# Border work of halves and layers in interleaved pieces, neighbouring seven-product units in alternation, last slabs in pairs

## The chip, the cores and the metric

The kernel runs on one core of a Trainium2 chip. The core has TensorE (PE, matrix products into the PSUM banks; PEld is its loading of weights), VectorE (DVE), ScalarE (ACT), GpSimd (POOL) and SyncE (SP, which issues the transfers from memory). Each engine works through its own list of instructions in order, and waits at an instruction until what it needs is there. The metric is the time of the whole program on the device in microseconds (us); lower is better.

## The reference

One inference step of a small encoder: 1024 frames of a new stream and 32 frames of a running one pass through two layers. Each layer is a mixer (Mamba-2 in the first, HGRN2 in the second) with a residual sum, then a gated feed-forward network (FFN) with a residual sum:

```python
def swiglu(h, w_gate, w_up, w_down):
    return (jax.nn.silu(h @ w_gate) * (h @ w_up)) @ w_down
...
            x = x + out.astype(x.dtype)
            x = x + swiglu(rmsnorm(x, ffn_norm_w[layer]), ffn_w_gate[layer], ffn_w_up[layer], ffn_w_down[layer])
        y = rmsnorm(x, final_norm_w)
```

The width is 1024, the FFN's hidden width 2816, all in float32. `rmsnorm` divides each frame by the root of its mean square and multiplies by a weight per channel.

## The kernel before

**Data.** The 1056 frames are two halves: h = 0 with 512 columns, h = 1 with 544, worked as two blocks of 272 (`BLK`). Channels lie on the 128 partitions, so `acc[h][m]`, m = 0 to 7, holds the residual stream. Every float32 operand is split into a rounded high part and a low rest (`xh`, `xl`; `wh`, `wl`), and a product is three matmuls: h by wh (L278), l by wh (L279), h by wl (L280). ACT makes the high part of a split by a copy, DVE the low part by a subtraction.

**The FFN.** Its hidden width is cut into eleven slabs of 256. The first slabs of a half (two of h = 0, one of h = 1) are done in the plain way (`ffn_head`: `ffn_up` twice, then `ffn_down`). The others are groups of slabs in `ffn_half`: for each slab a gate unit, then an upper unit; then the product with `w_down`, due after the next group's first gate unit. A group of two slabs (a pair) makes eight outputs of four k-steps, 12 matmuls each, where two single slabs make sixteen outputs of 6. Each output is added to `acc` by DVE (`acc<-mm,acc`), which frees its PSUM bank.

**A unit** (`ffn_unit`, `unit_weights`, `part`; L906 to L908) computes two blocks of 128 hidden channels by seven products of half the size in place of eight, with sums of the weights and of the inputs. Each of the parts p1, p5, p6, p3, p7, p2, p4 is 12 matmuls of half the columns (256 or 272). p1, p6, p7 and p4 go one after another into one PSUM bank, `px`, and between them ACT copies its state out (`s<-mm`); p5 and p3 go into `py`, p2 into `pz`. The sums of the weights are made on DVE as a unit goes on; its 1 MB of weights lands in a buffer of its own for one unit, and in two of the three `raw` buffers for the next. All other weights use those three as well.

**Border work.** Before a half's units can run, three things are needed: `x_stat` (the squares of `acc` on ACT, their sum on DVE, a product with ones on PE at L295, then rstd on ACT, kept in `rkeep`), the normed and split input (`xf`, then `h` and `l`), and `x_combos`, which makes from the channels k and k + 4 the sums for the seven products (`xt`) and splits them (`th`, `tl`). For the second half `x_combos` does the norm too.

**What sets the order.** A scheduler lists the instructions of each engine in the order of the program, except that work marked as raised moves ahead: `x_stat` and `x_combos` carry `@lifted("norm")`, a priority raised by 600. PSUM tiles come from a ring of five (`mm`) and a ring of three (`sc`); a product waits until the tile five, or three, before its own has been emptied. SP issues transfers in its list's order too, and waits when the buffer of one isn't free.

Of the kernel before, what the change touches and what calls it, by code (L numbers as in the profile page):

```python
# [47 lines left out]
def trunk_kernel(ctx, tc, x_prompt, x_sample, state_ssd, cache_conv, state_hgrn,  # L48
# [26 lines left out]
    def psum_mm():  # L75
        return pm.tile([P, 512], F32, tag="mm", bufs=5, name=nm("mm"))
# [751 lines left out]
    @lifted("norm")  # L828
    def x_stat(h, tag):

        keep = T(tag, "rkeep")
        return rstd_of([acc[h][m][:, :LEN[h]] for m in range(KD)], BLK[h], 1.0 / D, LEN[h], keep)

    @lifted("norm")
    def x_combos(h, wc, xn, tx, r=None):
# [3 lines left out]
        for k in range(4):  # L839
            xf = []  # L840
            for m in (k, k + 4):
                f = T("n", "xf")
                if xn[m] is not None:
                    tt(f[:, :L], xn[m][0].bitcast(F32)[:, :L], xn[m][1].bitcast(F32)[:, :L], ADD)
                else:
                    stt(f[:, :L], acc[h][m][:, :L], vc[:, wc + m:wc + m + 1], r[:, :L], MUL, MUL)
                    xn[m] = split(f[:, :L], L, (T("xn", "h", F32R), T("xn", "l", F32R)))
                xf.append(f)
# [6 lines left out]
            for q, f in enumerate((t, u)):  # L855
                tags = [XN2[4 * k + 2 * q], XN2[4 * k + 2 * q + 1]]
                tx[2 * k + q] = split(f[:, :L], L, (T(tags[0], "th", F32R), T(tags[1], "tl", F32R)))

# [17 lines left out]
    def unit_weights(src):  # L876
# [33 lines left out]
    def ffn_unit(h, src, xn, tx, dst):  # L910

        n = LEN[h] // 2
        w1, w5, w6, w3, w7, w2, w4 = unit_weights(src)
# [14 lines left out]
        part(py, n, w3, of(xn[4:], 1), True)  # L928
        tt(dst[0][:, hi], py[:, :n], s12[:, hi], ADD)
        part(px, n, w7, of(t34, 0), True)  # L930
        act(s35[:, lo], px[:, :n], AF.Copy)
        part(pz, n, w2, of(xn[4:], 0), False)
        tt(dst[0][:, lo], pz[:, :n], s12[:, lo], ADD)
        tt(dst[1][:, hi], s35[:, lo], s35[:, hi], ADD)
        part(px, n, w4, of(t34, 1), True)
        act(dst[1][:, lo], px[:, :n], AF.Copy)

    def ffn_gate(layer, h, s, xn, tx, g):
        L = LEN[h]
        g += [T("w", "fg") for _ in range(2)]  # L940
        ffn_unit(h, ffn_w_gate[layer][:, s * 256:(s + 1) * 256], xn, tx, g)
        for x in g:
            t = T("w", "ft")
            act(t[:, :L], x[:, :L], AF.Tanh, scale=0.5)
            stt(x[:, :L], t[:, :L], 1.0, x[:, :L], ADD, MUL)

    def ffn_upper(layer, h, s, xn, tx, g, hid):
        L = LEN[h]
        u = [T("xd", "fu") for _ in range(2)]
        ffn_unit(h, ffn_w_up[layer][:, s * 256:(s + 1) * 256], xn, tx, u)  # L950
        for x, y in zip(g, u):
            stt(y[:, :L], x[:, :L], 0.5, y[:, :L], MUL, MUL)
            hid.append(split(y[:, :L], L, (T("ys", "fh", F32R), T("ys", "fl", F32R))))
# [20 lines left out]
    def ffn_down(layer, h, s, hid, blocks=None, mid=None):  # L974
# [13 lines left out]
        if blocks is None:  # L988
            for c in range(nk):
                w = load(c)  # L990
                for m in range(c * cols // P, (c + 1) * cols // P):
                    for (b0, bn) in BLK[h]:
                        out(w, m, b0, bn)
# [7 lines left out]

    def ffn_head(layer, h, s, xn):

        hid = []
        return [lambda i=i: ffn_up(layer, h, s, i, hid, xn) for i in range(2)] + \
               [lambda: ffn_down(layer, h, s, hid)]
# [23 lines left out]
    def mixer_ffn(mixer, layer, wc, nxt):  # L1030
# [10 lines left out]
        for t in rest:  # L1041
            t()
# [126 lines left out]
```

## Time and profile before

| what | value |
|---|---|
| time, three runs | 3002.16, 2997.96, 2999.59 us (median 2999.59) |
| the profiled execution | 2997.74 us, its span 2996.0 us |
| PE busy | 2874.4 us (96%) |
| DVE busy | 2221.6 us (74%) |
| ACT busy | 1560.8 us (52%) |
| mean granted clock of the PE | 0.988 |

The rows shown further on come from the page of one profiled execution (busy times, groups of instructions, transfers) and from views of its trace: what an engine waited for (total us, times, longest), the timeline (start, length, engine, line, operation, output and inputs, shapes, count, and in brackets the idle time before it with what ended it), and stretches of the span with busy times by engine and the granted clock. L12 is line 12 of the kernel. Places on the timeline are us from the start of the span. Successive instructions overlap by a little, so the time between two starts is shorter than one's length.

In order of time the FFN of the first layer is at 930 to 1630 us (half border near 1250), that of the second at 2270 to 2950 (half border near 2585); the mixers lie before each.

### The profile page before, as it was taken

Reading aid. Unit: us, or ns where it says so; the run is one execution under the profiler, and the core shown is the slowest. Engines: PE = TensorE matmul, PEld = TensorE weight load, DVE = VectorE, ACT = ScalarE, POOL = GpSimd, SP = SyncE. Lnnn points to the kernel's source line nnn. Section 1 sums busy time; section 2 is a strip of 40 time slices with the busy share of each in tenths; the row PEclk is TensorE's granted clock in tenths of the full one; section 3 lists DMA queues with packets and bytes.
Section 4 is the critical chain, followed back from the end, with each engine's and each line's share of the span. In section 5 each row is a group of like instructions: output and inputs, shape, how many; then the busy total and the mean of one; then the engine's idle time right before and its main releaser. Section 6 shows DMA issues by size and latency. Waiting matters only on the chain.

```text
span 2996.0 us, 49501 instructions
## 1 busy us (share of the span) xinstructions
PE 2874.4 (96%) x19655; PEld 2625.4 (88%) x19655; DVE 2221.6 (74%) x3863; ACT 1560.8 (52%) x2928; POOL 51.9 (2%) x156
## 2 busy tenths in 40 slices
PE   7999999999998999899999999999999999899998
PEld 6777778989987998799999888899988999799998
DVE  6877787777787977977778555655568878787777
ACT  6745545553643644544444555655565545454445
POOL 0000000000100000000000000000000000000000
PEclk9999999999999999999999999999999999999999
DMA  5443324343332333222332222222222323333223
GB/s 143 121 109 102 99 71 127 107 114 96 100 97 78 105 114 92 89 81 87 112 92 76 85 78 81 68 76 76 77 77 91 113 85 99 95 99 92 85 88 106
DMA packets 398275, 283.42 MB, mean 95 GB/s; under 512 B 28873, under 2 KB 380634, under 8 KB 398042
## 3 DMA queue, kind: packets, MB, share of 16 engines
q1 hardware_dynamic: 398042, 280.25, 32.3%
q8 instruction: 154, 2.52, 0.4%
q14 instruction: 79, 0.65, 0.1%
HBM read 272.39 MB, written 7.82 MB: 94 GB/s over the span
## 4 chain that ended last, share of the span: by engine, by line
PE 71%; DVE 13%; DMA 7%; ACT 6%; issue 2%; SPq 0%; DVEq 0%; POOL 0%; ACTq 0%; POOLq 0%
PE mm L278 16%; PE mm L280 16%; PE mm L279 16%; PE mm L906 5%; PE mm L907 5%; PE mm L908 5%; DMA cumB<-cumd 2%; DMA raw<-in_ffn_w_gate_dram 2%; DVE wh L85 2%; ACT wh L82 1%; DMA raw<-in_ffn_w_up_dram 1%; ACT cumB L82 1%; PE sc L505 1%; PE sc L295 1%; PE sc L516 1%
## 5 line engine op out<-in xcount | busy, mean ns | idle before, releaser
L82 ACT ACTIVATE wh<-raw 128x512 fp32r<-128x512 f32 (+1 forms) x688 | 561.3, 819 | 762.9 <-PE mm L279 602.7
L278 PE MATMUL mm<-h,wh 128*128 128x272 f32 (+2 forms) x2064 | 676.0, 329 | 8.5 <-ACT h L82 4.0
L280 PE MATMUL mm<-h,wl 128*128 128x272 f32 (+2 forms) x2064 | 669.6, 325 | 2.7 <-DVE wl L85 2.7
L279 PE MATMUL mm<-l,wh 128*128 128x272 f32 (+2 forms) x2064 | 668.6, 324 | 1.2 <-DVE l L85 0.9
L85 DVE TENSOR_TENSOR wl<-raw,wh 128x1024 fp32r<-128x1024 f32 x308 | 376.3, 1223 | 141.5 <-ACT wh L82 123.5
L278 PEld LDWEIGHTS mm<-h,wh 128*128 128x128 f32 x2064 | 390.2, 189 | 39.3 <-ACT h L82 5.1
L280 PEld LDWEIGHTS mm<-h,wl 128*128 128x128 f32 x2064 | 390.6, 189 | 33.3 <-DVE wl L85 4.0
L279 PEld LDWEIGHTS mm<-l,wh 128*128 128x128 f32 x2064 | 390.6, 189 | 31.4 <-DVE l L85 3.0
L85 DVE TENSOR_TENSOR acc<-mm,acc 128x272 f32<-128x272 f32 (+1 forms) x544 | 278.3, 527 | 164.6 <-PE mm L280 162.4
L278 PE MATMUL mm<-fh,wh 128*128 128x272 f32 (+1 forms) x1056 | 346.0, 328 | 22.0 <-DVE acc L85 20.4
L906 PE MATMUL mm<-th,wh 128*128 128x272 f32 (+1 forms) x1216 | 351.8, 289 | 7.2 <-ACT s L82 6.6
L280 PE MATMUL mm<-fh,wl 128*128 128x272 f32 (+1 forms) x1056 | 343.9, 326 | 5.8 <-DVE wl L85 5.8
L907 PE MATMUL mm<-tl,wh 128*128 128x272 f32 (+1 forms) x1216 | 346.0, 285 | 0.0
L908 PE MATMUL mm<-th,wh 128*128 128x272 f32 (+1 forms) x1216 | 345.7, 284 | 0.0
L279 PE MATMUL mm<-fl,wh 128*128 128x272 f32 (+1 forms) x1056 | 345.2, 327 | 0.0
L85 DVE TENSOR_TENSOR wh<-raw,wh 128x512 fp32r<-128x512 f32 x380 | 257.2, 688 | 30.5 <-ACT wh L82 27.8
L906 PEld LDWEIGHTS mm<-th,wh 128*128 128x128 f32 x1216 | 228.7, 188 | 18.4 <-ACT s L82 18.1
L278 PEld LDWEIGHTS mm<-fh,wh 128*128 128x128 f32 x1056 | 200.7, 190 | 38.7 <-ACT wh L82 21.2
L908 PEld LDWEIGHTS mm<-th,wh 128*128 128x128 f32 x1216 | 229.1, 188 | 0.0
L907 PEld LDWEIGHTS mm<-tl,wh 128*128 128x128 f32 x1216 | 228.8, 188 | 0.0
L280 PEld LDWEIGHTS mm<-fh,wl 128*128 128x128 f32 x1056 | 201.1, 190 | 23.2 <-DVE wl L85 7.6
L279 PEld LDWEIGHTS mm<-fl,wh 128*128 128x128 f32 x1056 | 201.3, 191 | 15.5 <-DVE fl L85 0.5
(256 smaller groups left out, 5504.3 us busy)
## 6 DMA issues: line engine op xcount, KB each, us to landing
raw<-in_ffn_w_down_dram SPq DMA_DIRECT2D x90, 512.0 KB, 3.5
raw<-in_ffn_w_gate_dram SPq DMA_DIRECT2D x88, 512.0 KB, 4.8
raw<-in_ffn_w_up_dram SPq DMA_DIRECT2D x88, 512.0 KB, 3.8
raw<-in_ssd_in_w_dram SPq DMA_DIRECT2D x80, 512.0 KB, 4.5
raw<-in_hgrn_in_w_dram SPq DMA_DIRECT2D x64, 512.0 KB, 4.2
cumB<-cumd SPq DMA_DIRECT2D x64, 256.0 KB, 4.0
raw<-in_ssd_out_w_dram SPq DMA_DIRECT2D x32, 512.0 KB, 3.9
raw<-in_hgrn_out_w_dram SPq DMA_DIRECT2D x16, 512.0 KB, 3.3
```

The costliest lines, as they stand in the source:

```text
L82: A.activation(out=out, in_=in_, func=f, **kw)
L85: (eng or V).tensor_tensor(out=out, in0=a, in1=b, op=op)
L278: PE.matmul(ps[:, :bn], a, mh, start=(k == 0), stop=False)
L279: PE.matmul(ps[:, :bn], a, ml, start=False, stop=False)
L280: PE.matmul(ps[:, :bn], b, mh, start=False, stop=(k == n - 1))
L295: PE.matmul(ps[:, :bn], ones, tot[:, b0:b0 + bn], start=True, stop=True)
L505: PE.matmul(pp, Btok[:n, :], xw[:n, :], start=True, stop=True)
L516: PE.matmul(y13[r:r + 64, i // 2, :n], xdt[:n, i * 64:(i + 1) * 64], cums[i // 4][:n, i % 4, :n], start=True, stop=True)
L906: PE.matmul(ps[:, :n], a, mh, start=(k == 0 and not more), stop=False, skip_group_check=True)
L907: PE.matmul(ps[:, :n], a, ml, start=False, stop=False, skip_group_check=True)
L908: PE.matmul(ps[:, :n], b, mh, start=False, stop=(k == 3), skip_group_check=True)
```

## The change

1. `x_stat` and `x_combos` lose the raised priority. The norm of the second half leaves `x_combos` and becomes `norm_pieces`, one piece for a channel block and a block of columns. `x_combos`, `ffn_outs` (the outputs of `ffn_down`) and `ffn_head` return lists of pieces too; `mixed` interleaves two lists, `run` runs one. `x_stat` of the next half is called by `hook`, in the second group's first gate unit, after the outputs of the group before.
2. A unit becomes a generator that stops five times: p1 | p5, p2 | p6, p3 | p7 | p4 with what follows the unit. `in_turn` runs two neighbouring units A and B in the order A3 B1 A4 B2 A5, then B3 C1 B4 C2 B5, and so on. The sums of weights are made part by part. `px` comes from two `mm` banks of its own, `py` and `pz` from the `sc` ring of three, the outputs from the other three `mm` banks.
3. The last two slabs of a half are one pair, except at the end of the program, where they stay two singles.

```diff
-    def psum_mm():
-        return pm.tile([P, 512], F32, tag="mm", bufs=5, name=nm("mm"))
+    def psum_mm(among=(0, 1, 2, 3, 4)):
+        turn[0] += 1
+        i = among[turn[0] % len(among)]
+        return pm.tile([P, 512], F32, tag=f"mm{i}", bufs=1, name=nm("mm"))
...
-    @lifted("norm")
     def x_stat(h, tag):
...
-    @lifted("norm")
-    def x_combos(h, wc, xn, tx, r=None):
+    def norm_pieces(h, wc, out, blocks, r):
+
+        def piece(m, b0, bn):
+            xf = T("n", "xf")
+            stt(xf[:, :bn], acc[h][m][:, b0:b0 + bn], vc[:, wc + m:wc + m + 1], r[:, b0:b0 + bn], MUL, MUL)
+            if m == len(out):
+                out.append((T("xn", "h", F32R), T("xn", "l", F32R)))
+            xh, xl = out[m]
+            act(xh[:, b0:b0 + bn], xf[:, :bn], AF.Copy)
+            tt(xl[:, b0:b0 + bn], xf[:, :bn], xh[:, b0:b0 + bn].bitcast(F32), SUB)
+        return [lambda m=m, b=b: piece(m, *b) for b in blocks for m in range(KD)]
...
+        px = psum_mm((0, 1))
...
-        part(px, n, w1, of(xn[:4], 0), False)
+        part(px, n, next(w), of(xn[:4], 0), False)
         act(s12[:, lo], px[:, :n], AF.Copy)
-        part(py, n, w5, of(t12, 0), False)
+        yield
+        py, pz = psum_sc(), psum_sc()
+        part(py, n, next(w), of(t12, 0), False)
         act(s35[:, hi], py[:, :n], AF.Copy)
-        part(px, n, w6, of(t12, 1), True)
+        part(pz, n, next(w), of(xn[4:], 0), False)
+        yield
...
+    def in_turn(units):
+
+        step = lambda u: u and next(u, None)
+        prev = None
+        for u in list(units) + [None]:
+            if u:
+                u = u()
+            if prev is None:
+                step(u)
+                step(u)
+            else:
+                step(prev)
+                step(u)
+                step(prev)
+                step(u)
+                step(prev)
+            prev = u
...
+            ps = psum_mm((2, 3, 4))
+            product(ps, ws[c], (m * P) % cols, hid, b0, bn)
+            accumulate(h, m, ps, b0, bn)
+        return [lambda m=m, b=b: piece(m, *b) for m in range(KD) for b in BLK[h]]
...
-        groups = [1] * (n % 2) + [2] * ((n - 2) // 2) + [1, 1] if n % 2 == 0 else \
-                 [1] + [2] * ((n - 3) // 2) + [1, 1]
...
+        n = NSLAB - first - sum(tail)
+        groups = [1] * (n % 2) + [2] * (n // 2) + tail
...
-        due = ffn_half(layer, 0, xn[0], tx[0], HEAD)
-        due[0]()
-        x_combos(1, wc, xn[1], tx[1], r)
-        due[1]()
-        for t in ffn_head(layer, 1, 0, xn[1]):
-            t()
...
+        run(mixed(rest, tc0[2:3]))
+        run(mixed(h1[2:], tc0[3:]))
+        r = []
+        due = ffn_half(layer, 0, xn[0], tx[0], HEAD, lambda: r.append(x_stat(1, "ec")), [2])
+        run(mixed(ffn_outs(*due[0]), norm_pieces(1, wc, xn[1], BLK[1], r[0])))
+        tc1 = x_combos(1, xn[1], tx[1])
+        h2 = ffn_head(layer, 1, 0, xn[1])
+        run(h2[:1] + tc1[:1] + h2[1:2] + tc1[1:2] + mixed(h2[2:], tc1[2:]))
```

**How instructions move, first place.** DVE at the half border of the first layer (`acc_0_98` to `acc_7_105` are the first half's residual, `acc_..._106` to `_113` the second's; `mm` is an output in PSUM). Before:

```order
L85 TENSOR_TENSOR xt_12963<-xf_12951 128x272
L85 TENSOR_TENSOR l_12960<-xf_12957,h_12959 128x544
L85 TENSOR_TENSOR xt_12963<-xf_12957,xt_12963 128x272
L85 TENSOR_TENSOR xt_12964<-xf_12957,xf_12951 128x272
L85 TENSOR_TENSOR xt_12964<-xf_12957,xt_12963 128x272
L85 TENSOR_TENSOR fl_12789<-fu_12658,fh_12788 128x512
L85 TENSOR_TENSOR tl_12970<-xt_12963,th_12969 128x544
L85 TENSOR_TENSOR fl_12794<-fu_12659,fh_12793 128x512
L85 TENSOR_TENSOR tl_12974<-xt_12964,th_12973 128x544
L85 TENSOR_TENSOR acc_0_98<-mm_12803,acc_0_98 128x512
L85 TENSOR_TENSOR acc_1_99<-mm_12811,acc_1_99 128x512
```

And in the changed program:

```order
L92 SCALAR_TENSOR_TENSOR xf_12881<-acc_5_111,vc,rkeep_10366 128x272
L92 SCALAR_TENSOR_TENSOR xf_12901<-acc_6_112,vc,rkeep_10366 128x272
L89 TENSOR_TENSOR acc_0_98<-mm_12803,acc_0_98 128x512
L89 TENSOR_TENSOR l_12884<-xf_12881,h_12883 128x272
L92 SCALAR_TENSOR_TENSOR xf_12907<-acc_7_113,vc,rkeep_10366 128x272
L89 TENSOR_TENSOR acc_1_99<-mm_12829,acc_1_99 128x512
L89 TENSOR_TENSOR l_12904<-xf_12901,h_12903 128x272
L89 TENSOR_TENSOR wl_12916<-raw_12913,wh_12915 128x1024
L89 TENSOR_TENSOR l_12910<-xf_12907,h_12909 128x272
L92 SCALAR_TENSOR_TENSOR xf_12933<-acc_0_106,vc,rkeep_10366 128x272
L89 TENSOR_TENSOR acc_2_100<-mm_12861,acc_2_100 128x512
```

Before, the emptying of the first `mm` (`acc_0_98<-mm_12803`) stands behind all of the second half's norm and sums; now it stands between blocks of the norm, and the sums follow later, between outputs of the head.

**Second place.** ACT in the last gate and upper units of the first half (`s<-mm` copies out a unit's `px`, `s<-sc` or `s_2060_12559<-mm_12556` its `py`; `wh` and `fh` are splits). Before:

```order
L82 ACTIVATE s_2059_12558<-mm_12555 128x256
L82 ACTIVATE s_2060_12559<-mm_12556 128x256
L82 ACTIVATE wh_12665<-raw_12660 128x512
L82 ACTIVATE s_2059_12558<-mm_12555 128x256
L82 ACTIVATE wh_12669<-s_2067_12664 128x512
L82 ACTIVATE wh_12674<-raw_12660 128x512
L82 ACTIVATE s_2060_12559<-mm_12555 128x256
L82 ACTIVATE wh_12678<-s_2067_12664 128x512
L82 ACTIVATE wh_12681<-raw_12660 128x512
```

And in the changed program (`mm_12481` is the gate unit's `px`, `mm_12619` the upper unit's):

```order
L86 ACTIVATE s_2040_12482<-mm_12481 128x256
L86 ACTIVATE wh_12694<-raw_2042_12484 128x512
L86 ACTIVATE wh_12721<-raw_12622 128x512
L86 ACTIVATE s_2060_12620<-mm_12619 128x256
L86 ACTIVATE wh_12738<-s_2064_12626 128x512
L86 ACTIVATE s_2041_12483<-mm_12481 128x256
L86 ACTIVATE wh_12754<-raw_12622 128x512
L86 ACTIVATE ft_12710<-fw_12581 128x512
L86 ACTIVATE s_2061_12621<-sc_12660 128x256
```

Before, one `px`, `mm_12555`, is copied out again and again, with one other part between two uses; now the copies of two units' `px` alternate.

**Third place.** SP, the weights of a group of the first half. Before:

```order
L94 DMA raw_12249<-in_ffn_w_down_dram 128x4x256
L94 DMA raw_1988_12117<-in_ffn_w_gate_dram 128x4x256 x2
L94 DMA raw_12283<-in_ffn_w_down_dram 128x4x256
L94 DMA raw_12317<-in_ffn_w_down_dram 128x4x256
L94 DMA raw_2047_12526<-in_ffn_w_gate_dram 128x4x256 x2
L94 DMA raw_12351<-in_ffn_w_down_dram 128x4x256
L94 DMA raw_12387<-in_ffn_w_up_dram 128x4x256
L94 DMA raw_12388<-in_ffn_w_up_dram 128x4x256
```

And in the changed program:

```order
L98 DMA raw_12213<-in_ffn_w_up_dram 128x4x256
L98 DMA raw_1983_12075<-in_ffn_w_gate_dram 128x4x256 x2
L98 DMA raw_12214<-in_ffn_w_up_dram 128x4x256
L98 DMA raw_12307<-in_ffn_w_down_dram 128x4x256
L98 DMA raw_2042_12484<-in_ffn_w_gate_dram 128x4x256 x2
L98 DMA raw_12341<-in_ffn_w_down_dram 128x4x256
L98 DMA raw_12375<-in_ffn_w_down_dram 128x4x256
L98 DMA raw_12409<-in_ffn_w_down_dram 128x4x256
L98 DMA raw_12622<-in_ffn_w_up_dram 128x4x256
```

Before, the `w_up` loads follow the `w_down` loads; now those of an upper unit stand ahead of the `w_down` loads that the gate unit before it triggers.

More of the change, by code (lines that the diff above doesn't have):

```diff
@@ L842, in x_combos @@
                 f = T("n", "xf")
[L843 to L847, printed above, removed]
+                tt(f[:, :L], xn[m][0].bitcast(F32)[:, :L], xn[m][1].bitcast(F32)[:, :L], ADD)
                 xf.append(f)
@@ L988, in ffn_down @@
         if blocks is None:
[L989 to L993, printed above, removed]
+            for t in ffn_outs(layer, h, s, hid):
+                t()
         else:
@@ L1019, in ffn_half @@
                 g = []
-                ffn_gate(layer, h, s + i, xn, tx, g)
-                if i == 0 and gi < len(groups) - 1:
-                    for d in due:
-                        d()
-                    due = []
-                ffn_upper(layer, h, s + i, xn, tx, g, hid)
-            due.append(lambda s=s, hid=hid, **k: ffn_down(layer, h, s, hid, **k))
+                before = []
+                if i == 0 and gi <= len(groups) - len(tail):
+                    before, due = due, []
@@ L1027, in ffn_half, with gate @@
+                def gate(s=s + i, g=g, before=before, gi=gi):
+                    yield from ffn_gate(layer, h, s, xn, tx, g)
+                    for d in before:
+                        run(ffn_outs(*d))
+                    if gi == 1 and before:
+                        hook()
+                units.append(lambda gate=gate: gate())
+                units.append(lambda s=s + i, g=g, hid=hid: ffn_upper(layer, h, s, xn, tx, g, hid))
+            due.append((layer, h, s, hid))
             s += ng
+        in_turn(units)
@@ L1047, in mixer_ffn @@
-        r = x_stat(1, "ec")
-        due = ffn_half(layer, 0, xn[0], tx[0], HEAD)
-        due[0]()
-        x_combos(1, wc, xn[1], tx[1], r)
-        due[1]()
-        for t in ffn_head(layer, 1, 0, xn[1]):
-            t()
-        r = nxt and x_stat(0, "ss")
-        due = ffn_half(layer, 1, xn[1], tx[1], 1)
-        return due, r
+        xn, tx = [[], []], [[None] * KD, [None] * KD]
+        h0, h1 = [ffn_head(layer, 0, s, xn[0]) for s in range(HEAD)]
+        rest = mixer([lambda: norm(0, wc, xn[0], XN)] + h0[:2])
@@ L1058, in trunk_kernel @@
+        r = []
+        due = ffn_half(layer, 1, xn[1], tx[1], 1, lambda: r.append(nxt and x_stat(0, "ss")),
+                       [2] if nxt else [1, 1])
+        return due, r[0]
     wrow = []
```

122 lines of the change are left out of this document (66 added, 56 removed).

## The prediction

> **What bounds the kernel now.** I read the busy times first, then what TensorE (PE) waited for, then the places on its timeline, then the clock.
>
> ```profile
> PE 2874.4 (96%) x19655; PEld 2625.4 (88%) x19655; DVE 2221.6 (74%) x3863; ACT 1560.8 (52%) x2928; POOL 51.9 (2%) x156
> PE mm L278 <- DVE acc L85: 23.5, 3, 10.2
> PE mm L906 <- ACT s L82: 6.6, 13, 0.9
> ```
>
> The PE is the bound: 96% of the span, no other engine over 74%. Since the change issues as many matmuls as before, of the same sizes, only its waits and its clock can move the end. The waits are few and large: the one on `acc` happens three times and costs 23.5 us. The timeline of the PE says where. A number in brackets is the wait ahead of that row and its releaser.
>
> ```profile
> 963.96 2.18 PE L295 MATMUL sc<-sq,ones 128*128 128x272 f32 x4 [10.17 <-DVE sq L85]
> 1252.97 0.76 PE L278 MATMUL mm<-fh,wh 128*128 128x512 f32 x1 [10.23 <-DVE acc L85]
> 1256.41 0.79 PE L280 MATMUL mm<-fh,wl 128*128 128x512 f32 x1 [2.24 <-DVE wl L85]
> 1625.17 0.39 PE L278 MATMUL mm<-fh,wh 128*128 128x272 f32 x1 [0.53 <-DVE fu L85]
> 1627.23 0.40 PE L278 MATMUL mm<-fh,wh 128*128 128x272 f32 x1 [1.05 <-DVE nco L1120]
> 1631.57 0.60 PE L280 MATMUL mm<-fh,wl 128*128 128x272 f32 x1 [1.32 <-DVE wl L85]
> 2280.05 0.60 PE L278 MATMUL mm<-hy,wh 128*128 128x272 f32 x1 [3.06 <-DVE acc L85]
> 2284.32 0.40 PE L280 MATMUL mm<-hy,wl 128*128 128x272 f32 x1 [0.56 <-DVE wl L85]
> 2583.16 0.77 PE L278 MATMUL mm<-fh,wh 128*128 128x512 f32 x1 [10.20 <-DVE acc L85]
> 2586.60 0.79 PE L280 MATMUL mm<-fh,wl 128*128 128x512 f32 x1 [2.24 <-DVE wl L85]
> ```
>
> Five places, each a border where norms and sums for the seven products fall due: the first layer's FFN head (964), its half border (1253), the layer border (1625), the second FFN's head (2280), its half border (2583). The ten waits add up to 41.6 us. VectorE (DVE) is what is late; its timeline at 1253 shows why.
>
> ```profile
> 1225.09 1.48 DVE L88 SCALAR_TENSOR_TENSOR xf<-acc,vc,rkeep 128x544 f32<-128x544 f32 x2
> ...
> 1237.91 0.45 DVE L85 TENSOR_TENSOR xt<-xf,xt 128x272 f32<-128x272 f32 x1
> 1238.27 0.45 DVE L85 TENSOR_TENSOR xt<-xf,xf 128x272 f32<-128x272 f32 x1
> ...
> 1251.49 0.74 DVE L85 TENSOR_TENSOR tl<-xt,th 128x544 fp32r<-128x544 f32 x1
> 1252.12 3.10 DVE L85 TENSOR_TENSOR acc<-mm,acc 128x512 f32<-128x512 f32 x5
> 1255.11 1.24 DVE L85 TENSOR_TENSOR wl<-raw,wh 128x1024 fp32r<-128x1024 f32 x1
> ```
>
> From 1225 to 1252 the DVE does the raised `x_combos` of the next half and empties none of the five `mm` banks; then it empties five in a row. The PE filled them and stood still.
>
> The clock adds to it. The columns of the stretches are length; PE, weight load, DVE, ACT and POOL busy; granted clock; DMA share and GB/s.
>
> ```profile
> 964.00:970.00 6.00, 6.00 (x16) 4.72 (x17) 3.56 (x7) 2.91 (x4) 0.00 (x0) 0.57 0.00 0
> 1252.50:1260.00 7.50, 4.78 (x12) 3.38 (x13) 7.50 (x11) 0.20 (x1) 0.00 (x0) 0.55 0.27 76
> 1626.00:1636.00 10.00, 7.63 (x40) 7.13 (x39) 9.80 (x20) 3.32 (x4) 0.00 (x0) 0.66 0.33 92
> 2279.00:2285.00 6.00, 4.38 (x21) 4.17 (x22) 5.97 (x12) 4.53 (x6) 0.00 (x0) 0.72 0.01 3
> 2582.00:2590.00 8.00, 4.60 (x10) 3.23 (x11) 8.00 (x12) 0.89 (x1) 0.00 (x0) 0.50 0.24 70
> 1000.00:1225.00 225.00, 223.94 (x1549) 206.85 (x1548) 181.94 (x298) 114.72 (x221) 0.00 (x0) 1.00 0.33 101
> 1300.00:1610.00 310.00, 306.29 (x2413) 302.53 (x2412) 238.22 (x411) 149.46 (x283) 0.00 (x0) 1.00 0.30 89
> ```
>
> Busy time times lost clock, row by row: 6.00 x 0.43 = 2.6, 4.78 x 0.45 = 2.2, 7.63 x 0.34 = 2.6, 4.38 x 0.28 = 1.2, 4.60 x 0.50 = 2.3, together 10.9 us. The borders so cost 41.6 + 10.9 = **52.5 us**. The last two rows are stretches of units: clock 1.00, and 530.2 of 535 us busy.
>
> **Part 1, the border work in pieces.** What leaves is the solid block of DVE work; the same operations come back, cut into pieces between products. For the half border I counted both written orders. Steps from start to start on the DVE, out of the rows above and the next one: a 544-wide operation 0.63 (1251.49 to 1252.12), 272 wide 0.36 (1237.91 to 1238.27), 512 wide 0.61 (a fifth of the 3.10, less the tail), a wide `wl` 1.13 (1255.11 to 1256.24); the `xf` scaling 0.74 at 544, and half, 0.37, at 272.
>
> ```profile
> 1256.24 0.71 DVE L85 TENSOR_TENSOR acc<-mm,acc 128x512 f32<-128x512 f32 x1
> ```
>
> For the matmuls two pairs of rows give the steps: 512 columns 0.23 us, 272 columns 0.125 (0.13 in this pair; twelve of them take 1.5).
>
> ```profile
> 946.46 0.39 PE L280 MATMUL mm<-fh,wl 128*128 128x512 f32 x1
> 946.69 0.40 PE L278 MATMUL mm<-fh,wh 128*128 128x512 f32 x1
> ...
> 1342.32 0.29 PE L907 MATMUL mm<-tl,wh 128*128 128x272 f32 x1
> 1342.45 0.29 PE L908 MATMUL mm<-th,wh 128*128 128x272 f32 x1
> ```
>
> Before, in the worst stretch, the DVE owes 4 `xf`, 12 operations of 544, 14 of 272, 10 of 512 and 2 `wl`: 3.0 + 7.6 + 5.0 + 6.1 + 2.3 = 24.0 us, against 28 matmuls of 512 columns, 6.4 us. The excess is 17.6 us. The two waits there are 12.5 us and the clock's 2.2 between them, so some 3 us were covered by work already filled in. At the head the same count gives an excess of 12.0 for a wait of 10.2, a cover of 1.8. After, the worst stretch of the half border (sums of the seven products among the first slab's outputs) has 31 operations of 272 (16 emptied banks, 12 sums, 3 others), 8 of 544, 4 of 512 and one `wl`: 11.2 + 5.0 + 2.4 + 1.1 = 19.7 us against 132 matmuls of 272 columns, 16.5. The excess falls to 3.2. The same count gives 3.1 at the first head, 3.4 at the layer border (before, 7.9 for waits of 2.9: a cover of 5.0) and 1.7 at the second head (before, 10.2 for 3.6, a cover of 6.6). If the covers stay, a wait of 1.3 remains at the first head, 0.3 to 0.4 at each half border, and none elsewhere. A short wait still costs clock in this trace (0.66 at 1626, where no wait is over 1.32), so I charge a slow clock of 2.6 at the first head and half of one at each half border: 1.3 + 2.6 + 2 x (0.4 + 1.3) = **7 us remain**, with bounds 0 (all covered) and 5 x (1.5 + 2.6) = 20. The gain is **45.5 us**, between 32 and 52.5.
>
> The Trainium skill ("TensorE: Matmul & The Clock Gate", "HAM oscillation — how this bites in real kernels") says that it is PE gaps over some 3.4 us that bring the slow clock. By that rule the waits left over would cost their 2.1 us alone, not 7, and the sum would end 5 us lower. The trace does not agree: its 0.66 at 1626 comes with waits of 1.05 and 1.32 us.
>
> **Part 2, alternating products.** In a unit `px` serves p1, p6, p7 and p4, and only one other part (12 matmuls, 1.5 us) lies between two uses. When ACT's queue is longer, the PE waits:
>
> ```profile
> 1341.16 0.28 PE L908 MATMUL mm<-th,wh 128*128 128x272 f32 x1
> 1342.09 0.39 PE L906 MATMUL mm<-th,wh 128*128 128x272 f32 x1 [0.65 <-ACT s L82]
> 1342.32 0.29 PE L907 MATMUL mm<-tl,wh 128*128 128x272 f32 x1
> ...
>   ACT s L82: 24.7, 66
> ```
>
> The last row is what L906 waited for with the weight loads counted in (66 times); the table of PE waits has 6.6. From 1341.16 to 1342.09 are 0.93 us where 0.125 is due: 0.8 lost where 0.65 is booked as wait, so 6.6 is too little; 24.7 counts some waits twice. Alternating puts two parts (3.0 us) in between at each turn, which covers every wait seen; the gain is that wait whole. I take the middle, **16 us** (6.6 to 24.7). Clock there is 1.00 already, so it brings nothing more.
>
> The skill's same page ("A second HAM failure mode: psum-queue depth-cycling") holds that frequent micro-idles between groups of matmuls make the clock swing. By it, ending them would also win clock; the granted clock of 1.00 in the two stretches with those idles says there is none to win.
>
> **Part 3, the sums of squares (`x_stat`) in the units.** It now comes three times within gate units: 8 squares on ACT, 7 additions on DVE, one or two matmuls, two activations with a change of table each way. Behind the squares on ACT stand copies of `px`, for which the PE waits. One square and one table load take:
>
> ```profile
> L82 ACT ACTIVATE sq<-acc 128x544 f32<-128x544 f32 x24 | 14.9, 651 | 7.3 <-DVE acc L85 5.3 <-DVE sq L85 0.8 <-DVE xt L85 0.8
> L82 ACT ACT_TABLE_LOAD x96 | 123.2, 1283 | 17.8 <-DVE hec L683 8.2 <-DVE hlg L85 7.2 <-PEq L1156 0.8
> ```
>
> That is 8 x 0.65 + 2 x 1.28 = 7.8 us of ACT per place, spread over parts in which ACT is busy half the time; by the order the excess there is 2.6 to 2.8 us, the cover two parts, 3.0. I charge 1 us each, **+3** (0 to 8, at 2.7 each).
>
> **Part 4, paired last slabs, and split norms.** At three places eight outputs of 12 matmuls replace 16 of 6. That saves 8 + 16 + 8 emptied banks on the DVE; the norm cut into blocks of 272 adds about as much again. Both are inside the counts above: 0. Weights move the same bytes.
>
> Sum: -45.5 - 16 + 3 = **-58.5 us**. From the profiled 2997.7 this gives 2939.2; the median of the runs shown lies 1.9 above the profiled one, so **2941**. With best and worst ends: -77 to -30, or 2922 to 2969.
>
> **Rivals.**
>
> *Half-filled borders.* The DVE's order is fixed, and a bank behind a sum of squares or a split that itself waits for ACT keeps the PE as now, only shorter. Two waits of 1.2 us and one slow clock (2.6) at each border are 25 us; alternation brings only the recorded 6.6, and the hooks cost 8. The result is -52.5 + 25 - 6.6 + 8 = -26, 2974. For it: the layer border, where short waits cost the clock. Against: DVE is idle for a fifth of the unit stretches (181.94 of 225 us busy), and its excess per border falls to a third or less. Chance 0.18.
>
> *Down weights through one buffer (slower).* `raw` has three buffers. In the changed order the up unit's two loads are issued ahead of the gate's outputs, and stay until that unit's weights are split; the four `w_down` loads of a pair then pass through the third one, one by one.
>
> ```profile
> raw<-in_ffn_w_down_dram SPq DMA_DIRECT2D x90, 512.0 KB, 3.5
> L82 ACT ACTIVATE wh<-raw 128x1024 fp32r<-128x1024 f32 x308 | 324.7, 1055 | 453.0 <-PE mm L279 384.3 <-DMA raw<-in_ssd_in_w_dram 22.5 <-PE mm L908 18.5
> ```
>
> One turn takes 3.5 (landing) + 1.06 (`wh`) + 1.24 (`wl`, shown above) = 5.8 us plus queueing; the PE uses a load in 24 x 0.23 = 5.5 or 48 x 0.125 = 6.0. The first load can start some four parts (5.7 us) early, so a turn of 7.4 still starves nobody. It decides from 58.5 / 14 = 4.2 us per pair (14 pairs lie inside gates): a wait of 1.6 plus a slow clock of 2.6, so a turn of about 8. At 9 it loses 3 x 3.5 - 5.7 + 2.6 = 7.4 at 6 pairs of the first half and 3 x 3 - 5.7 + 2.6 = 5.9 at 8 of the second: 92 in all, +33, **3033**. Against it: more than 2 us of queueing per turn would be needed, with ACT half idle. Chance 0.07.
>
> *All cover holds.* Nothing remains at the borders or the hooks, and alternation brings 24.7: 2922 or below. Chance 0.10.
>
> *The waits only move.* Without the raised priority the scheduler might put the norm's pieces late, and the next product waits for `h` instead of for a bank. The written order shows them early; 2995 to 3000. Chance 0.03.
>
> **How the numbers follow.** The forecast, 2941, has 0.62. About 0.2% (6 us) is what a measurement of this kernel tells from no change. Faster: the forecast, half-filled borders and full cover, less a little of the second for worse luck: 0.88. Same 0.05, slower 0.07. The range of 8 in 10 takes the forecast's own 2922 to 2969, a little of full cover below and most of the half-filled case above: 2918 to 2978.
>
> **What would show it.** Right: no wait of 10 us on `acc` or `sq` in the PE's waits; the granted clock at the borders near 1; the L906 wait on ACT `s` nearly gone; PE busy down by some 10 us (clock) and its share at 98%. Wrong: waits of L278 or L280 on `wl` in the gate units would speak for the single buffer; waits of 1 to 2 us at the borders with clocks of 0.6 to 0.8 for half-filled ones; waits on `s` beside squares for the hooks.

## The result and the profile after

The changed kernel takes 2944.91 us (median of four runs, 2942.06 to 2945.21), the kernel before 2998.78 beside it: a ratio of 0.9818 with a 95% interval of 0.9801 to 0.9835, so 49 to 60 us faster. The forecast was 2941 (2918 to 2978). Timed once more, on the chip of a later series, the ratio was 0.9805 (0.9792 to 0.9818). The kernel before took 5 to 7 us less in the later series than in the first, so ratios are compared from here on; 0.001 is 3 us.

The busy times of the changed kernel, then the main lines of the FFNs among what its PE waited for (total us, times, longest). L282 to L284 are the three matmuls of a plain product, L917 to L919 those of a unit's part.

```profile
PE 2855.9 (97%) x19655; PEld 2618.4 (89%) x19655; DVE 2205.6 (75%) x3879; ACT 1551.3 (53%) x2944; POOL 52.7 (2%) x156
```

```profile
PE mm L282 <- DVE fxd L89: 7.8, 7, 2.1
PE sc L299 <- DVE sq L89: 5.4, 8, 1.5
PE mm L284 <- DVE wl L89: 3.6, 6, 1.0
PE mm L919 <- DVE wh L89: 2.7, 3, 1.3
PE mm L282 <- DVE acc L89: 0.9, 3, 0.4
PE mm L917 <- ACT s L86: 0.4, 2, 0.2
```

The waits of 10 us on `acc` and `sq` are gone: 23.5 us on `acc` became 0.9, and the longest wait left in the FFNs' products is 2.1. A new line heads them, products waiting for DVE's `fxd`, seven times. With its weight loads counted in, the first matmul of a part now waits little for ACT:

```profile
  ACT fw L86: 2.6, 4
  ACT s L86: 2.0, 8
```

Before, `s` stood there with 24.7 us and 66 times. The stretches (length; PE, weight load, DVE, ACT, POOL busy; clock; DMA share, GB/s) at the five borders, two stretches of units, and one place behind a wait:

```profile
940.00:965.00 25.00, 24.15 (x150) 20.93 (x150) 23.93 (x46) 11.76 (x22) 0.00 (x0) 1.00 0.08 22
1210.00:1285.00 75.00, 72.73 (x491) 66.90 (x490) 67.83 (x132) 32.80 (x61) 0.00 (x0) 1.00 0.27 82
1585.00:1640.00 55.00, 54.08 (x347) 49.00 (x347) 36.61 (x62) 23.66 (x35) 0.00 (x0) 1.00 0.40 115
2215.00:2240.00 25.00, 25.00 (x125) 21.09 (x124) 20.47 (x38) 10.50 (x15) 0.00 (x0) 1.00 0.28 84
2565.00:2590.00 25.00, 23.23 (x181) 22.58 (x180) 24.57 (x51) 11.02 (x21) 0.00 (x0) 1.00 0.08 22
965.00:1205.00 240.00, 238.29 (x1683) 222.54 (x1683) 195.75 (x326) 129.05 (x250) 0.00 (x0) 1.00 0.33 101
1345.00:1530.00 185.00, 184.59 (x1469) 183.72 (x1468) 143.38 (x251) 92.81 (x175) 0.00 (x0) 1.00 0.30 92
1335.00:1342.00 7.00, 5.41 (x31) 5.41 (x32) 6.11 (x11) 3.56 (x6) 0.00 (x0) 0.76 0.31 96
```

All five borders run at the full clock (0.50 to 0.72 before). On DVE the emptied banks (`acc<-mm,acc`) now stand among the norm's pieces at the first half border:

```profile
1224.37 0.50 DVE L92 SCALAR_TENSOR_TENSOR xf<-acc,vc,rkeep 128x272 f32<-128x272 f32 x1
1224.79 0.69 DVE L89 TENSOR_TENSOR acc<-mm,acc 128x512 f32<-128x512 f32 x1
1225.39 0.43 DVE L89 TENSOR_TENSOR l<-xf,h 128x272 fp32r<-128x272 f32 x1
1225.73 1.32 DVE L92 SCALAR_TENSOR_TENSOR xf<-acc,vc,rkeep 128x272 f32<-128x272 f32 x3
1226.97 0.44 DVE L89 TENSOR_TENSOR l<-xf,h 128x272 fp32r<-128x272 f32 x1
1227.48 0.69 DVE L89 TENSOR_TENSOR acc<-mm,acc 128x512 f32<-128x512 f32 x1
```

To compare places I use one sum, made from all matmul records of a trace: the time between the starts of two successive matmuls, less the median of this for the first one's shape. It counts waits, refilling and slow clock alike. Where exactly the stretches are cut moves a sum by 1 or 2 us.

| lost by the PE, us | five borders | stretches of units | whole program |
|---|---|---|---|
| before | 56.8 | 27.2 | 189.8 |
| changed, first profile | 11.6 | 19.3 | 132.5 |
| changed, second profile | 11.5 | 12.1 | 123.1 |

The work at full cadence is some 2792 us before and 2793 after, so the whole gain is in these losses: 45 us at the borders, 8 to 15 among the units, and 4 to 6 elsewhere. That the two profiles of one kernel differ by 7 us among the units is taken up with the last experiment.

### The profile page after: what moved, and what is told of

Same layout as the page of the kernel before. It is cut to its first block, busy times and chain, and to the rows that moved or that the text cites. A ratio compares the mean times of both kernels' runs of the same rounds, so it can differ in the third digit from the quotient of the medians.

```text
span 2940.3 us, 49353 instructions
## 1 busy us (share of the span) xinstructions
PE 2855.9 (97%) x19655; PEld 2618.4 (89%) x19655; DVE 2205.6 (75%) x3879; ACT 1551.3 (53%) x2944; POOL 52.7 (2%) x156
## 4 chain that ended last, share of the span: by engine, by line
PE 75%; DVE 12%; DMA 6%; ACT 5%; issue 2%; SPq 0%; DVEq 0%; POOL 0%; ACTq 0%; POOLq 0%
PE mm L282 16%; PE mm L284 16%; PE mm L283 16%; PE mm L919 3%; PE mm L917 3%; PE mm L918 3%; PE sc L919 3%; PE sc L917 3%; PE sc L918 3%; DMA cumB<-cumd 3%; DMA raw<-in_ffn_w_gate_dram 2%; DVE wh L89 2%; ACT wh L86 1%; PE sc L509 1%; ACT cumB L86 1%
## 5 line engine op out<-in xcount | busy, mean ns | idle before, releaser
L86 ACT ACTIVATE wh<-raw 128x512 fp32r<-128x512 f32 (+1 forms) x688 | 554.2, 817 | 592.4 <-PE mm L283 363.3
L282 PE MATMUL mm<-h,wh 128*128 128x272 f32 (+2 forms) x2064 | 675.0, 328 | 7.9 <-ACT h L86 3.9
L284 PE MATMUL mm<-h,wl 128*128 128x272 f32 (+2 forms) x2064 | 668.5, 324 | 2.7 <-DVE wl L89 2.7
L282 PEld LDWEIGHTS mm<-h,wh 128*128 128x128 f32 x2064 | 390.0, 189 | 38.1 <-ACT h L86 4.9
L284 PEld LDWEIGHTS mm<-h,wl 128*128 128x128 f32 x2064 | 390.2, 189 | 33.0 <-DVE wl L89 3.9
L282 PE MATMUL mm<-fh,wh 128*128 128x272 f32 (+1 forms) x1056 | 343.2, 326 | 8.9 <-DVE fxd L89 7.8
L89 DVE TENSOR_TENSOR acc<-mm,acc 128x272 f32<-128x272 f32 (+1 forms) x512 | 259.6, 524 | 110.3 <-PE mm L284 107.6
L284 PE MATMUL mm<-fh,wl 128*128 128x272 f32 (+1 forms) x1056 | 341.1, 324 | 0.6 <-DVE wl L89 0.6
L917 PE MATMUL mm<-th,wh 128*128 128x272 f32 (+1 forms) x912 | 260.9, 286 | 0.4 <-ACT s L86 0.4
L919 PE MATMUL mm<-th,wh 128*128 128x272 f32 (+1 forms) x912 | 259.6, 285 | 0.2 <-DVE wh L89 0.2
L918 PE MATMUL mm<-tl,wh 128*128 128x272 f32 (+1 forms) x912 | 259.6, 285 | 0.0
L282 PEld LDWEIGHTS mm<-fh,wh 128*128 128x128 f32 x1056 | 198.8, 189 | 26.9 <-DVE fxd L89 9.3
L284 PEld LDWEIGHTS mm<-fh,wl 128*128 128x128 f32 x1056 | 199.5, 189 | 16.1 <-DVE wl L89 1.0
L917 PE MATMUL sc<-h,wh 128*128 128x272 f32 (+1 forms) x608 | 173.7, 286 | 0.5 <-ACT wh L86 0.5
L917 PEld LDWEIGHTS mm<-th,wh 128*128 128x128 f32 x912 | 171.7, 188 | 2.5 <-ACT s L86 1.7
L919 PE MATMUL sc<-h,wh 128*128 128x272 f32 (+1 forms) x608 | 173.3, 285 | 0.0
```

Source lines behind the costliest of these rows:

```text
L86: A.activation(out=out, in_=in_, func=f, **kw)
L89: (eng or V).tensor_tensor(out=out, in0=a, in1=b, op=op)
L282: PE.matmul(ps[:, :bn], a, mh, start=(k == 0), stop=False)
L284: PE.matmul(ps[:, :bn], b, mh, start=False, stop=(k == n - 1))
L917: PE.matmul(ps[:, :n], a, mh, start=(k == 0 and not more), stop=False, skip_group_check=True)
L918: PE.matmul(ps[:, :n], a, ml, start=False, stop=False, skip_group_check=True)
```

## The experiments

### Units in sequence, weights part by part

```diff
-            if prev is None:
...
-                step(prev)
-                step(u)
-                step(prev)
...
+        for u in units:
+            for _ in u():
+                pass
```

with the parts in their old order. Expected:

> The changed kernel, with the parts of a unit in their old order and the units one after another; the border pieces, the hooks and the pairs stay. Theory of the forecast: alternation is worth the px waits, 16 us (6.6 to 24.7), so 2945 + 16 = 2961 us (2952 to 2970), and the PE waits of the seven-product lines on ACT s come back to some 6.6 us. Rival, from the trace of the changed kernel: alternation also brought the seven waits of a product on DVE fxd (7.8 us, and a slow clock after one of them), so undoing it gives some of its gain back and costs only about 8 us, 2953, with those seven waits gone.

Measured: 0.9834 (0.9821 to 0.9848), 5 us over the first timing of the changed kernel and 9 over the second, the intervals touching in part. The units lose 16.1 us, the borders 12.3, the whole 132.4, as the changed kernel's first profile. The first matmul of a part waits more for ACT's `s` than in the changed kernel, 9.8 us against 2.0, but far less often than before (12 times, not 66):

```profile
  ACT s L86: 9.8, 12
  ACT wh L86: 8.0, 6
```

So alternation is worth less than its 16 us: something else had removed most of these waits. The rival was closer, at 8 us, and in the table of PE waits `fxd` no longer shows.

### Old borders

```diff
+    @lifted("norm")
     def x_stat(h, tag):
...
+        run(ffn_outs(*due[0]))
+        x_combos(1, wc, xn[1], tx[1], r)
+        run(ffn_outs(*due[1]))
+        run(ffn_head(layer, 1, 0, xn[1]))
```

> The changed kernel with the border work as before (x_stat and x_combos raised, norm of the second half inside x_combos, last slabs single); units still alternate. Theory: the border work is worth 45.5 us, so 2945 + 45 = 2990 us (2977 to 2999), with three PE waits of about 10 us back and the granted clock at the borders near 0.55. Rival, that alternation brought most and the pieces little: 2960 or less. If the two parts add up, this run's gain on the kernel before and that of the run with units in sequence together make the 54 us.

Measured: 1.0011 (1.0002 to 1.0020). Without the pieces nothing of the gain is left. The units lose only 10.9 us, but the borders 73.4 against 56.8 before. At the first half border stands one wait of 17.29 us, where the kernel before had 10.23 and 2.24:

```profile
1254.46 0.79 PE L284 MATMUL mm<-fh,wl 128*128 128x512 f32 x1 [17.29 <-DVE wl L89]
```

The two parts don't add: with solid border work, what alternation and its order of weights win among the units (16 us) is lost at the borders (17 us). Whether this comes from the alternation, or from the output banks being three by name instead of five, this run doesn't tell.

### Single last slabs

```diff
-        due = ffn_half(layer, 0, ..., lambda: r.append(x_stat(1, "ec")), [2])
+        due = ffn_half(layer, 0, ..., lambda: r.append(x_stat(1, "ec")), [1, 1])
```

and the same for the other two pairs.

> The changed kernel with the last two slabs single again at three places (sixteen outputs of 6 matmuls in place of eight of 12). Theory of the forecast: nothing, since the border's DVE work stays below the PE's: 2945 us (2941 to 2949). Rival: the 32 more emptied banks (8 x 0.61 at two borders with 512 columns or 16 x 0.36 each) land in the stretches where DVE and PE are nearly even, and the PE waits for about a half of them: 2950 to 2960, with waits on acc at the borders.

Measured: 0.9830 (0.9816 to 0.9843), 4 to 7 us above the changed kernel, at the edge of what intervals from two series can tell. The borders lose 15.7 us instead of 11.6, about 2.5 at each half border. The forecast's nothing and the rival's half of 15 us are both a little off; the pairs bring some 4 us by the trace.

### Statistics at the border

```diff
-                    if gi == 1 and before:
-                        hook()
...
         in_turn(units)
+        hook()
```

> The changed kernel with x_stat called after the last unit of a half instead of within the second group's gate unit. Theory: the hook costs 3 us in the units, but at the border the norm pieces wait for 8 squares, their sum, a product and two activations, about 8 us at three borders: 2945 - 3 + 24 = 2966 us (2950 to 2970). The wait of 2.1 us at 1336 in the changed kernel, and the slow clock behind it, should then be gone if the squares cause it; rival: that wait comes from weights of the next gate unit that land late and hold up DVE, and it stays (there are others like it without a hook, at 1540 and 2841).

Measured: 0.9859 (0.9846 to 0.9873), 12 to 16 us slower; the theory had 21. The borders lose 27.1 us, 15 more, and the first half border shows why: the head waits for its `wh`, behind norm pieces that themselves waited for the statistics.

```profile
1245.45 0.46 PE L282 MATMUL mm<-h,wh 128*128 128x272 f32 x1 [3.88 <-ACT wh L86]
```

The units lose 13.7 us, within what the changed kernel's two profiles lose with the hook (12.1 and 19.3): the hook's own cost is too small to see. And where the changed kernel had its wait near 1336, DVE still stands here, with no squares about:

```profile
1344.79 0.69 DVE L89 TENSOR_TENSOR s<-raw 128x512 f32<-128x512 f32 x1 [2.10 <-DMA raw<-in_ffn_w_gate_dram]
```

The product behind it still waits for `fxd`, 1.41 us in place of 2.10, and at the full clock. So the rival holds for that wait: the weights of the next gate unit land late.

### What removed the waits on px

A second theory was formed: in the kernel before, a unit's seven weights were summed and split ahead of its first part, and ACT's copies of `px` stood behind these splits; the changed kernel makes them part by part (`next(w)`). Three kernels separate this from alternation, with the changed kernel beside them.

> The changed kernel itself, as the measure for the runs beside it: a ratio to the kernel before of 0.982, as in its first timing (0.9818).

Measured: 0.9805 (0.9792 to 0.9818).

```diff
-        w = unit_weights(src)
+        w = iter(list(unit_weights(src)))
```

> The changed kernel, but each unit's seven weights are summed and split before its first part, as in the kernel before, instead of part by part; units alternate. Theory A, of the forecast: the px waits go because two parts lie between two uses, so with alternation it makes no difference, ratio 0.982 (about 2945 us on the scale of the first timing). Theory B, formed from the run with units in sequence: the copies of px stood behind a unit's own weight splits in ACT's list, and making these part by part is what removed the waits; then 10 to 20 us come back, ratio 0.985 to 0.989, with waits on ACT s or wh in the unit lines.

Measured: 0.9831 (0.9817 to 0.9844), 8 us above the changed kernel; the units lose 21.2 us. The waits on `s` stay few, though, with the weight loads counted in 4.6 us in 8 places. So most of the loss lies in something other than the wait that Theory B names, and what it is stays open.

The same line in the kernel with units in sequence:

> As the run of units in sequence, but with a unit's seven weights made before its parts, so that the units are as in the kernel before while the border pieces stay. Theory A: 16 us over the changed kernel (6.6 to 24.7), ratio 0.987, against 0.983 for the run in sequence with weights part by part only if that order matters too. Theory B: the same 0.987 to 0.990 here, with the loss of some 20 us in the unit stretches back. If neither is at work, 0.983 and small losses in the unit stretches: then the five-bank ring that px shared with the outputs is left as the cause.

Measured: 0.9863 (0.9849 to 0.9876), 17 us above the changed kernel; the units lose 27.0 us, as much as before the change, though the borders (13.1) are in pieces. The waits are back, 58 times where the kernel before has 66:

```profile
  ACT s L86: 19.8, 58
  ACT wh L86: 8.9, 6
```

Last, the kernel before with the part-by-part weights alone:

```diff
-        w1, w5, w6, w3, w7, w2, w4 = unit_weights(src)
+        w = unit_weights(src)
...
-        part(px, n, w1, of(xn[:4], 0), False)
+        part(px, n, next(w), of(xn[:4], 0), False)
```

> The kernel before with one part of the change alone: the weights of a unit are made part by part; no alternation, no border pieces, the same ring of banks. Theory A: no difference, ratio 1.000 (0.998 to 1.002). Theory B: the px waits go here too, 15 to 20 us, ratio 0.993 to 0.995, with the border waits of 10 us as before.

Measured: 0.9957 (0.9944 to 0.9969), 13 us faster than before, with neither alternation nor border pieces. Its units lose 9.9 us in place of 27.2, its borders 59.0 as ever. Two stretches, its waits, and the row of `s` with the weight loads counted in (24.7 us and 66 times in the kernel before):

```profile
1000.00:1220.00 220.00, 219.40 (x1538) 204.56 (x1537) 179.15 (x295) 112.95 (x218) 0.00 (x0) 1.00 0.31 100
1300.00:1600.00 300.00, 298.04 (x2378) 297.38 (x2378) 235.38 (x403) 147.80 (x280) 0.00 (x0) 1.00 0.29 92
```

```profile
PE mm L278 <- DVE acc L85: 25.2, 3, 12.3
PE sc L295 <- DVE sq L85: 15.5, 7, 10.2
PE mm L905 <- ACT s L82: 5.8, 8, 1.2
  ACT s L82: 13.5, 17
```

Put together (the run in sequence with weights part by part is of another series):

| ratio (us lost among the units) | weights first | weights part by part |
|---|---|---|
| units in sequence | 0.9863 (27.0) | 0.9834 (16.1) |
| units alternate | 0.9831 (21.2) | 0.9805 (12.1), 0.9818 (19.3) |

Either cure alone brings about half of the 17 us, 9 or 10, and the other then adds some 4 to 9. Each alone also takes most of the waits on `s`: 58 in the upper left kernel, 12 with weights part by part, 8 with alternation. So neither Theory A nor Theory B alone is the cause: the copies of `px` come late for a reason that each of the two weakens. The ring of banks is not that reason: the upper left kernel has the new banks and loses as much as the kernel before (27.0 and 27.2).

Where both cures meet, something new appears: weights that land late. In the changed kernel DVE waits 32.8 us for the gate units' weights and ACT 149.6 us for those of the outputs:

```profile
DVE s L89 <- DMA raw<-in_ffn_w_gate_dram: 32.8, 16, 3.5
ACT wh L86 <- DMA raw<-in_ffn_w_down_dram: 149.6, 41, 5.0
```

With units in sequence and weights part by part the two are 9.5 us and none, in the kernel before 12.1 and none, and with alternating units and weights first:

```profile
DVE s L89 <- DMA raw<-in_ffn_w_gate_dram: 0.5, 2, 0.3
ACT wh L86 <- DMA raw<-in_ffn_w_down_dram: 0.8, 1, 0.8
```

Little of this waiting reaches the PE (the waits on `fxd` below). Whether it is why the second cure adds less was not tried.

### Two halves of the border work

The pieces kept interleaved, with the raise put back on them:

```diff
+    @lifted("norm")
     def x_stat(h, tag):
...
+        piece = lifted("norm")(piece)
         return [lambda k=k: piece(k) for k in range(4)]
```

> The changed kernel with the raised priority of 600 put back on x_stat, the norm pieces and the pieces of x_combos; the written interleaving, alternation and pairs stay. Theory: the raise alone draws the pieces together ahead of the emptied banks, so most of the border loss returns: ratio to the kernel before 0.993 to 1.000, with PE waits of several us on acc or sq and a granted clock near 0.5 after them. Rival, that the interleaved writing is enough: 0.985 or less.

Measured: 0.9968 (0.9955 to 0.9980); the borders lose 55.5 us. And not raised, but written as whole blocks:

```diff
-        run(h2[:1] + tc1[:1] + h2[1:2] + tc1[1:2] + mixed(h2[2:], tc1[2:]))
+        run(tc1)
+        run(h2)
```

> The changed kernel without the interleaving: no raised priority, but outputs, norm, sums for the seven products and head are written as whole blocks one after another. Theory of the forecast: interleaving is what keeps the DVE's excess small at each place, so a block of norm and sums of some 15 us stands ahead of the head's emptied banks and 20 to 40 us come back: ratio 0.988 to 0.995. Rival: dropping the raise is all that matters, since the scheduler itself mixes work that is ready: 0.980 to 0.984.

Measured: 0.9948 (0.9934 to 0.9961); the borders lose 55.8 us. The longest wait at the first half border, of the raised pieces and then of the plain blocks:

```profile
1231.12 1.22 PE L282 MATMUL mm<-fh,wh 128*128 128x512 f32 x2 [7.58 <-ACT fh L86]
```

```profile
1257.79 0.59 PE L282 MATMUL mm<-h,wh 128*128 128x272 f32 x1 [9.81 <-ACT wh L86]
```

Each half alone leaves about the whole border loss of 56 us in place, with the wait on another tile. Only both together remove it. On DVE one sees the solid block in both runs: with the raise, nothing but pieces of norm and sums from 1219 to 1229 us; in plain blocks, nothing but sums and their splits from 1248 to 1259. So the raise undoes the interleaving, and without interleaving the block only stands later.

### The new wait on `fxd`

In the changed kernel the first product behind a gate unit waited up to 2.1 us for DVE's `fxd<-sc,s`, which empties the upper unit's `pz`. In the built program that product's bank was the one that `pz` had used: the names `mm0` to `mm4` and `sc` don't fix physical banks, tiles are laid where one is free, and both names occur in all eight banks. The rings of the description are rings by name only. DVE was late there for this reason:

```profile
1334.89 0.69 DVE L89 TENSOR_TENSOR s<-raw 128x512 f32<-128x512 f32 x1 [2.51 <-DMA raw<-in_ffn_w_gate_dram]
1335.50 0.68 DVE L89 TENSOR_TENSOR sq<-sq,sq 128x512 f32<-128x512 f32 x1
1336.10 0.44 DVE L89 TENSOR_TENSOR fxd<-sc,s 128x272 f32<-128x272 f32 x1
```

The sum of the next gate's weights stands ahead of `fxd` in DVE's order, and waited 2.51 us for the weights. All gate units share one buffer, so a load has to wait until DVE is through with the gate unit before: SP issued this one at 1329.33, after waiting 9.8 us for DVE, and DVE went on with the new weights at 1334.89. Eight PSUM tiles held for a whole half separate the two causes:

```diff
+        banks[:] = [pm.tile([P, 512], F32, tag=f"mm{i}" if i < 5 else "sc", bufs=1 if i < 5 else 3, name=nm("bank")) for i in range(8)]
         in_turn(units)
+        banks.clear()
```

> The changed kernel with eight PSUM tiles held for the length of a half's units, so that px, py and pz, and the outputs each keep banks of their own (in the changed program the packer laid the first output of a gate's products into a bank last used by a unit's pz). Theory: the first output no longer waits for the emptying of pz (DVE fxd), 4 to 8 us of waits go and the slow clock at 1336 with them: ratio 0.977 to 0.979. Rival: the DVE itself stands still there, waiting for the next gate unit's weights from memory, and the wait only moves to the next bank: 0.980 to 0.982, as the changed kernel.

Measured: 0.9809 (0.9796 to 0.9822). In this run two neighbouring units could share one `px`, as the next expectation says; the run below has it apart.

> As the run with eight held PSUM tiles, in which two neighbouring units could take the same px (so that products were added into one another, at the same amount of work); here the two px alternate on a counter of their own. That run showed no wait on DVE fxd any more and a ratio of 0.9809. Theory: 4 to 8 us of waits go, 0.977 to 0.979. Rival, that this wait was only the mark of a DVE that stands still for late weights, or too small to be told: 0.980 to 0.982 again, with the fxd waits gone from the trace.

Measured: 0.9825 (0.9811 to 0.9838). No product waits for `fxd`, and the ratio is no better. DVE stands for late gate weights again (1.88 us), and near it a product waits 2.53 us for a bank that DVE has not emptied. That wait has another origin, though: ahead of the emptying DVE waited for ACT's `wh`, and ACT 3.24 us for a `w_down` load:

```profile
1401.88 0.69 DVE L97 TENSOR_TENSOR s<-raw 128x512 f32<-128x512 f32 x1 [1.88 <-DMA raw<-in_ffn_w_gate_dram]
1404.70 1.06 ACT L94 ACTIVATE wh<-raw 128x1024 fp32r<-128x1024 f32 x1 [3.24 <-DMA raw<-in_ffn_w_down_dram]
1405.79 1.22 DVE L97 TENSOR_TENSOR wl<-raw,wh 128x1024 fp32r<-128x1024 f32 x1 [2.50 <-ACT wh L94]
```

```profile
1408.06 0.40 PE L290 MATMUL bank<-fh,wh 128*128 128x272 f32 x1 [2.53 <-DVE acc L97]
```

The rival holds in this: the waits on `fxd` go and the ratio stays, so the shared bank was not what cost the time. That late gate weights alone moved the wait to the next bank is not shown. The cost differs from one execution to the next: in the changed kernel's second profile the `fxd` waits are 4.4 us in place of 7.8, and no slow clock follows them, which is part of the 7 us between its two profiles. More room for the weights gave no result: a kernel with a fourth `raw` buffer was expected at 0.976 to 0.982, but it doesn't fit into the core's memory beside the rest, and that buffer would have served the upper units and `w_down`, not the gate units. No run was clearly faster than the changed kernel.

## Why the prediction was right, and where only by its sum

**The bound, and the border term.** That the PE is the bound and that five borders hold the loss was right, and the size too: 45.5 us forecast, 45.2 measured (56.8 to 11.6). That the two agree to 0.3 us is luck: the borders cost 4 us more than forecast before (56.8 against 52.5) and 5 more after (11.6 against 7, where the terms themselves add up to 7.3), and the two misses cancel. What was right for its reason is that the count of DVE against PE work left little over. Its composition was off. The 7 us that were to remain were 2 us of waits and 5 of slow clock; 11.6 remained, all of it short waits and refilling, at the full clock. The step that failed is "a short wait still costs clock". It was taken from the layer border, where 0.53 and 1.05 us fell into one step of the clock; at the changed kernel's borders no step holds more than 1.3 us of idle time, and none of their steps is slow (last section). Part 1 took the lost raise and the pieces as one thing. The runs show that neither brings anything at the borders without the other.

**The alternation term.** 16 us were forecast; the two edits to the units bring 13 to 17 by the timing (0.9863 to 0.9818 and 0.9805) and 8 to 15 by the trace. But the step "alternating puts two parts in between at each turn, which covers every wait seen; the gain is that wait whole" gave to alternation what it shares with the part-by-part weights, and took the gain for the wait: alternation without that edit takes the waits on `s` from 58 to 8, but only 6 of the 27 us that the units lose. The diff showed this edit, and I priced it at nothing without naming it; the description of the kernel before even has these sums made "as a unit goes on", where its code lists all seven ahead of the first part. Alone in the kernel before it brings 13 us; alternation without it brings 9.6 (0.9863 to 0.9831).

**Hooks.** Charged with 3 us; their own cost can't be told from none, and without them 12 to 16 are lost. The place near 1336 that would have been theirs was mostly late weights.

**Pairs and split norms.** Costed at 0; the pairs bring about 4 us at the borders by the trace, at the edge of the timing.

**Rivals.** *Half-filled borders* falls by the clock of 1.00 at all five. *All cover holds* falls by the 11.6 us. *The waits only move* is wrong for the change, though it is what each half of the border work alone does. *Down weights through one buffer* came true in its mechanism and not in its price: ACT now waits 41 times for a `w_down` load, and in the first layer the four loads of a pair are split 6.5 to 7.1 us apart on average, where the kernel before has 4.1 to 4.5. The forecast worked out a turn of 5.8 us plus queueing, and 7.4 as the turn that still starves nobody; nobody starves: the PE's waits of L284 on `wl` are 3.6 us in six places, 1.0 at most. The loads of the gate weights, not named in the forecast, come late too and hold DVE up.

The sum, -58.5 forecast and -53.9 measured (-49 to -60 by the interval), so came out partly by luck. The borders were right by two misses that cancel, the second term was near in size with half of its cause missed, a new wait of 4 to 8 us stands against some 5 us of slow clock that never came, and 4 to 6 us were won elsewhere, which no term had.

## What to carry to other kernels

Count, stretch by stretch, the work that an engine must finish before it empties the next bank, against the work the PE has in hand: that difference told that little would be left at the borders, where busy shares (74% on DVE before, 75% after) said nothing. Raised priority and interleaved writing work against each other, so take away the one when you write the other, and test each alone. In a diff with several edits give each its own price, also one that looks like a mere rewriting, such as a list turned into a generator: it moves work in the queues.

## What the runs showed of the hardware

The traces have the granted clock as full or half, and it changes only in steps of 3.41 us on a grid that stays in place through an execution. A clock of 0.76 over 7 us is one such step at half. Cut along this grid, the changed kernel's wait of 2.10 us (1336) lies within one step, and the next step is slow; its wait of 1.85 us (1540) lies across two, and neither slows the step behind it.

```profile
1336.59 0.40 PE L282 MATMUL mm<-fh,wh 128*128 128x272 f32 x1 [2.10 <-DVE fxd L89]
1334.40:1337.81 3.41, 1.31 (x10) 1.22 (x10) 2.85 (x5) 1.59 (x3) 0.00 (x0) 1.00 0.32 100
1337.81:1341.22 3.41, 3.41 (x17) 3.41 (x16) 2.81 (x4) 1.82 (x4) 0.00 (x0) 0.50 0.29 78
1540.21 0.39 PE L282 MATMUL mm<-fh,wh 128*128 128x272 f32 x1 [1.85 <-DVE fxd L89]
1535.78:1539.19 3.41, 2.58 (x21) 2.36 (x19) 0.08 (x1) 0.01 (x1) 0.00 (x0) 1.00 0.67 225
1539.19:1542.60 3.41, 2.39 (x19) 2.40 (x20) 2.69 (x4) 2.00 (x3) 0.00 (x0) 1.00 0.01 5
1542.60:1546.02 3.42, 3.42 (x30) 3.42 (x29) 1.87 (x5) 0.00 (x1) 0.00 (x0) 1.00 0.45 153
```

The first and fourth rows are waits on the PE's timeline, the others steps of the grid. So it isn't the length of a single wait that decides. In the run with plain blocks even a wait of 2.51 us costs no clock, because a boundary of the grid cuts it into 1.38 and 1.13:

```profile
1615.63 0.39 PE L282 MATMUL mm<-fh,wh 128*128 128x272 f32 x1 [2.51 <-DVE acc L89]
1611.09:1614.50 3.41, 2.03 (x17) 1.81 (x15) 3.41 (x6) 1.51 (x3) 0.00 (x0) 1.00 0.00 0
1614.50:1617.91 3.41, 2.28 (x18) 2.28 (x18) 3.41 (x9) 2.31 (x4) 0.00 (x0) 1.00 0.29 77
1617.91:1621.33 3.42, 2.50 (x20) 2.28 (x20) 3.42 (x4) 0.46 (x1) 0.00 (x0) 1.00 0.21 49
```

What goes with a slow step is the PE's idle time within the step before it, added up. In the two FFNs of all fourteen traces a step at the full clock with up to 1.5 us of it was never followed by a slow one (0 of 5618), one with 1.88 us or more always (31 of 31), and in between 4 of 10 were. A slow step was followed by a slow one whenever it held 0.64 us or more (47 of 47), and by none below (0 of 35). This also explains the layer border of the kernel before: 0.53 and 1.05 us fell into one step, 1.58 together, and the wait of 1.32 fell into the slow step behind it and kept the clock low for one more.

The Trainium skill ("TensorE: Matmul & The Clock Gate", "HAM oscillation — how this bites in real kernels") puts the gap at over some 3.4 us. The runs agree that short gaps cost no clock by themselves, but about half of that time, gathered within one step, is enough here.
